# Parking the scores of the last three dense tiles in DRAM, searching them beside the gate matrix, and moving the point that holds the gathers

## The chip, the cores and the metric

The kernel runs on one core of one Trainium2 chip. The metric is the device time of one execution in microseconds; of several runs the median counts. One execution was also profiled, and all rows below come from that one. The engines are called PE (TensorE, with its weight loads as PEld), DVE (VectorE), ACT (ScalarE), POOL (GpSimd) and SP (SyncE, which here only issues transfers); a "q" behind a name is that engine's instruction queue, where waits and issues stand.

## What is computed

One decoder layer on 1024 tokens of width 1024: retention and stick-breaking attention, an output projection, and then a feed-forward layer of 16384 single-neuron experts (PEER). The change lies in that last part:

```python
qry = (ht @ w_query).reshape(T, PEER_HEADS, 2, PEER_HALF)
sub_scores = jnp.einsum('thpc,hpkc->thpk', qry, sub_keys).astype(jnp.float32)
top_s, top_i = lax.top_k(sub_scores, K)                 # 8 heads x 2 halves, 128 keys, 16 kept
cand_s = top_s[:, :, 0, :, None] + top_s[:, :, 1, None, :]
best_s, best_c = lax.top_k(cand_s.reshape(T, PEER_HEADS, K * K), K)
gate = jax.nn.softmax(best_s, axis=-1)
# for each token: 128 experts (8 heads x 16)
a = jnp.einsum('pd,ped->pe', xb, expert_down[ids])
act = jax.nn.gelu(a, approximate=False) * gates
y = jnp.einsum('pe,ped->pd', act, expert_up[ids])
```

So each token has 16 rows of 128 scores, of each of which the 16 largest are wanted, and then a second choice among sums of pairs.

## The kernel before

The 1024 tokens are eight tiles of 128. Tiles 0 to 3 are *gathered*: for each of a token's 128 experts one indirect DMA on POOL fetches 128 rows of `down` (`row("down", j)`, line 778), DVE takes the inner product (line 789); then the same with `up` (line 778 again, and DVE's accumulation at line 799). That is 256 gathers of 512 KB for a tile, 1024 in all, numbered n = 256 t + j (128 more for `up`), through five buffers `g`. Tiles 4 to 7 are *dense*: all experts are computed for 512 tokens with matmuls, and a gate matrix that is zero for experts that were not chosen picks the right ones.

The order in which work is traced: three segments of attention and routing (`seg_gen`, tiles 0, 1 to 3, 4 to 7), then `dense`, then the gathers of all four tiles. A planner that simulates the engines orders the instructions of each engine: what is traced earlier goes first where both could go, so gathers fill gaps. Each engine then runs its list in order.

*Routing in a segment.* For each quarter g of the query weights (`stream(A["wq"], ...)`) PE forms queries and scores; ACT copies the scores of one half-head, for all tiles of the segment, into a tile `sco` of the segment's pool `v` (nine buffers). For a tile that has an entry in `sc_d` the scores go to DRAM with one transfer of 64 KB for each tile and half-head (line 649); before the change that is tile 3 alone. For the other tiles `top16` (lines 672 to 676, five DVE instructions) searches them at once. `topk` (lines 694 to 751) makes the second choice, with small DVE instructions and copies on ACT in between. For tile 4 (t0 == NG) it is called in four pieces of two heads, one behind each quarter; for tiles 5, 6 and 7 it is handed on in the list `late`, for eight heads at a time.

*The dense part.* First six experts' first halves (`stage1_ahead`, lines 836 to 839, their splits at line 824 on POOL), and `to_slots` for tile 4. Then the gate matrix, in 16 pieces c of 32 tokens: for each of eight steps q one DVE comparison (line 876, 128 x 1024), one POOL product (line 877), one ACT copy, PE products (line 883) and ACT copies out, and the piece is written to DRAM (`g_d`). Tile 4 takes pieces 0 to 3, tile 5 pieces 4 to 7, and so on. The pieces also carry 24 further `stage1_ahead` between them, whose splits (line 824) run on DVE. The late `topk` of tiles 5, 6 and 7 are traced before pieces 1, 5 and 9 (`LC`). Then come 32 groups of four blocks of 128 experts each: gate product (line 920), split (line 923), and the second matmuls (lines 946 to 948; 32 of line 946 in each group). Tile 3's parked scores are read back (line 680) and searched two heads at a time before groups 4, 5, 6 and 7 (`todo`, `route_late`).

*The hold.* Gathers with n from 480 to 495 may not be issued on POOL before the last POOL product of gate piece 4 (`HOLD`, `HOLD_C`, `tc.issue_after`); later ones follow them through the five buffers.

Of the kernel before, what the change touches and what calls it, by code (L numbers as in the profile page):

```python
# [23 lines left out]
NT = 8  # L24
SEGS = [(0, 1), (1, 3), (4, 4)]
NG = 4
# [4 lines left out]
LC = 1, 5, 9  # L31

RET = "h0 K h1 t0 Q h2 t1 V h3 t2 | t3"
HOLD, HOLD_C = 480, 4
LT0, LATE = 3, (4,)
# [19 lines left out]
def tile_kernel(ctx, tc, A, out):  # L55
# [10 lines left out]
    sc_d = {t: dram.tile([128, 16, 128], F32, name=f"scd{t}") for t in range(LT0, NG)}  # L66
# [163 lines left out]
    def seg_gen(phase, t0, nt, hooks):  # L230
# [403 lines left out]
        for g in range(4):  # L634
            ky = V((128, 4, 128))
            SP.dma_start(ky, A["keysT"][:, 4 * g:4 * g + 4])

            def ev_q(i, acc):
                q = V()
                copy(q[:, :n], acc[:, :n])  # L640
                tp = pstile("tp", 2)
                for j in range(nt):
                    PE.matmul(tp[:, 128 * j:128 * j + 128], q[:, 128 * j:128 * j + 128], ky[:, i], start=True, stop=True)
                sco = V()
                copy(sco[:, :n], tp[:, :n])
                for j in range(nt):
                    s, h, p = sco[:, 128 * j:128 * j + 128], (4 * g + i) // 2, i % 2
                    if t0 + j in sc_d:
                        SP.dma_start(sc_d[t0 + j][:, 2 * h + p, :], s)
                    else:  # L650
                        top16(kp, tv[j][:, h, p], ix[j][:, h, p], s)

            stream(A["wq"], 512 * g, hT[t0], ev_q, True)
            if t0 in (0, NG):
                topk(kp, tv[0][:, 2 * g:2 * g + 2], ix[0][:, 2 * g:2 * g + 2], t0, 2 * g, 2)
        if t0 == 0:
            return []
        late = []
        for i in own[t0 == NG:]:
            f = lambda i=i: topk(kp, tv[i], ix[i], t0 + i, 0, 8)  # L660
            if t0 < NG:
                f()
            else:
                late.append(f)
        return late
# [143 lines left out]
    def dense(Hhi, Hlo, dp, kpg, late):  # L809
# [50 lines left out]


        iota8 = iota128[:, None, :, :].to_broadcast([128, 2, 128, 4])
        for c in range(TD // CT):
            for k in range(1, 4):
                if c == LC[k - 1]:
                    late[k - 1]()
# [30 lines left out]
        todo = {g: (t, 2 * k) for t, gg in zip(sc_d, LATE) for k, g in enumerate(range(gg, gg + 4))}  # L897
# [84 lines left out]
    with tc.tile_pool(name="tp", bufs=1) as tp_:  # L982
        kpg = tc.tile_pool(name="kp", bufs=1, side="right")
        kp = kpg.__enter__()
        with tc.tile_pool(name="att", bufs=1) as att:
# [4 lines left out]
            with tc.tile_pool(name="wp", bufs=1) as wp, tc.tile_pool(name="up", bufs=13) as up, \  # L990
                    tc.tile_pool(name="vp", bufs=9) as vp:
                late = []
                for s in SEGS:
                    late = seg_gen((wp, tp_, up, vp, kp), *s, late)
        with tc.tile_pool(name="gr", bufs=1) as gr, tc.tile_pool(name="dp", bufs=1, reuse_waits="tile") as dp:
            hold = dense(*hT[NG], dp, kpg, late)
# [61 lines left out]
```

## Time and profile before

| | us |
|---|---|
| median of three runs | 3145.78 |
| the three runs | 3138.63 to 3146.57 |
| the profiled execution | 3142.38 |
| its span | 3140.7 |

Busy shares of the span: PE 86%, DVE 80%, POOL 61%, ACT 41%; mean granted PE clock 0.906. A busy share over the whole span mixes stages; the tables by stretch are what is read below. The stretches, in us from the span's start: 1320 to 1432 the query weights of the third segment, 1432 to 1476 the gap until the gate matrix, 1476 to 1792 the gate matrix, from 1840 the groups.

### The profile page before, as it was taken

To read this page: it belongs to the slowest core of one execution; us is meant where nothing else is said; L and a number is where in the kernel's file an instruction comes from. 1 tells how busy PE (TensorE), PEld (TensorE's weight loads), DVE (VectorE), ACT (ScalarE), POOL (GpSimd) and SP (SyncE) were. 2 spreads that over 40 slices of the span, in tenths; PEclk is the share of its full clock that TensorE was granted. 3 is DMA by queue.
4 is the path that set the end of the run, shared out by engine and by line. 5 is a ranking of instruction groups with operands and counts; after the bars stand their busy time and mean duration, and the time that the engine had idled before them with its cause. 6 is when DMAs were issued, how large, how long until landed. Compare 5 with 4: busy or idle time off the path is not lost.

```text
span 3140.7 us, 38200 instructions
## 1 busy us (share of the span) xinstructions
PE 2691.9 (86%) x12308; PEld 2091.2 (67%) x12308; DVE 2514.9 (80%) x4677; ACT 1287.2 (41%) x2255; POOL 1914.5 (61%) x1590
## 2 busy tenths in 40 slices
PE   6957877787987787794889999789999999999995
PEld 2454654576765345583778887667877788888884
DVE  2269879799988898899989867997666677788778
ACT  1223334244333363432666644444444444444441
POOL 1125775677787567751478757545666666766664
PEclk9978985888998588896999999899999999999998
DMA  8788877998787777960379889778998999998997
GB/s 321 251 302 275 299 236 255 319 358 291 252 289 246 251 237 261 325 228 28 115 286 353 320 303 348 255 256 314 324 333 306 331 341 338 338 338 331 352 338 261
DMA packets 299881, 903.36 MB, mean 288 GB/s; under 512 B 34840, under 2 KB 102424, under 8 KB 279200
## 3 DMA queue, kind: packets, MB, share of 16 engines
q0 software_dynamic: 147456, 536.94, 48.3%
q1 hardware_dynamic: 152224, 363.98, 32.2%
q8 instruction: 97, 1.59, 0.2%
q14 instruction: 104, 0.85, 0.1%
HBM read 848.34 MB, written 52.45 MB: 287 GB/s over the span
## 4 chain that ended last, share of the span: by engine, by line
PE 34%; DVE 27%; DMA 15%; issue 12%; POOL 9%; ACT 3%; SPq 1%; POOLq 0%; DVEq 0%; ACTq 0%
DMA g<-in_up_dram,ids 6%; DVE g L789 6%; POOL g L778 5%; PE tp L837 4%; PE tp L838 4%; PE tp L839 4%; PE acc L948 4%; PE acc L946 3%; PE acc L947 3%; DVE gy L799 3%; DMA g<-in_down_dram,ids 3%; DVE p L876 2%; PE acc L263 2%; POOL wlo L273 2%; DVE oh L736 1%
## 5 line engine op out<-in xcount | busy, mean ns | idle before, releaser
L778 POOL DMA_INDIRECT g<-in_down_dram,ids x512 | 549.7, 1074 | 446.0 <-DVE g L789 229.9
L778 POOL DMA_INDIRECT g<-in_up_dram,ids x512 | 562.2, 1098 | 383.4 <-DVE gy L799 253.7
L799 DVE SCALAR_TENSOR_TENSOR gy<-g,a,gy 128x1024 f32<-128x1024 f32 x508 | 651.3, 1282 | 100.2 <-DMA g<-in_up_dram,ids 94.8
L789 DVE SCALAR_TENSOR_TENSOR g<-g,gy 128x1024 f32<-128x1024 f32 x512 | 614.3, 1213 | 107.6 <-DMA g<-in_down_dram,ids 105.4
L837 PE MATMUL tp<-Thi,dhi 128*128 128x512 f32 x1024 | 407.7, 398 | 37.0 <-ACT dhi L71 30.5
L946 PE MATMUL acc<-u,p 128*128 128x512 f32 x1024 | 399.1, 399 | 27.0 <-ACT p L71 14.1
L948 PE MATMUL acc<-u,p 128*128 128x512 f32 x1024 | 386.5, 396 | 26.0 <-DVE p L923 26.0
L839 PE MATMUL tp<-Thi,dlo 128*128 128x512 f32 x1024 | 403.7, 395 | 3.1 <-DVE dlo L824 2.5
L947 PE MATMUL acc<-u,p 128*128 128x512 f32 x1024 | 405.0, 397 | 0.0
L838 PE MATMUL tp<-Tlo,dhi 128*128 128x512 f32 x1024 | 404.7, 395 | 0.0
L824 POOL TENSOR_TENSOR u<-raw,u 128x1024 fp32r<-128x1024 f32 x128 | 306.7, 2409 | 18.1 <-ACT u L71 16.4
L273 POOL TENSOR_TENSOR wlo<-wraw,whi 128x512 fp32r<-128x512 f32 x182 | 235.8, 1306 | 79.2 <-ACT whi L71 71.2
L824 DVE TENSOR_TENSOR dlo<-raw,dhi 128x1024 fp32r<-128x1024 f32 x122 | 200.2, 1642 | 87.3 <-ACT dhi L71 87.3
L71 ACT ACTIVATE whi<-wraw 128x512 fp32r<-128x512 f32 x208 | 128.3, 629 | 336.6 <-PE acc L283 117.6
L837 PEld LDWEIGHTS tp<-Thi,dhi 128*128 128x128 f32 x1024 | 195.5, 191 | 79.7 <-ACT dhi L71 32.6
L946 PEld LDWEIGHTS acc<-u,p 128*128 128x128 f32 x1024 | 197.1, 192 | 73.7 <-ACT p L71 17.3
L948 PEld LDWEIGHTS acc<-u,p 128*128 128x128 f32 x1024 | 194.8, 191 | 72.4 <-DVE p L923 32.1
L282 PE MATMUL acc<-wlo,Thi 128*128 128x512 f32 x504 | 212.5, 422 | 30.6 <-POOL wlo L273 30.5
L71 ACT ACTIVATE yacc<-acc 128x512 f32<-128x512 f32 x186 | 108.3, 592 | 296.2 <-PE acc L948 295.0
L839 PEld LDWEIGHTS tp<-Thi,dlo 128*128 128x128 f32 x1024 | 195.2, 191 | 44.8 <-DVE dlo L824 3.5
L947 PEld LDWEIGHTS acc<-u,p 128*128 128x128 f32 x1024 | 197.1, 192 | 41.4
L838 PEld LDWEIGHTS tp<-Tlo,dhi 128*128 128x128 f32 x1024 | 195.6, 191 | 39.3
(271 smaller groups left out, 5076.1 us busy)
## 6 DMA issues: line engine op xcount, KB each, us to landing
raw<-in_downT_dram SPq DMA_DIRECT2D x64, 1024.0 KB
raw<-in_up_dram SPq DMA_DIRECT2D x64, 1024.0 KB
gd<-u SPq DMA_DIRECT2D x32, 1024.0 KB
gm<-gd SPq DMA_DIRECT2D x512, 64.0 KB
wraw<-in_w_in_dram SPq DMA_DIRECT2D x56, 512.0 KB
u<-in_ada_w_dram SPq DMA_DIRECT2D x46, 512.0 KB
wraw<-in_wq_dram SPq DMA_DIRECT2D x32, 512.0 KB
u<-in_w_in_dram SPq DMA_DIRECT2D x28, 512.0 KB
```

The source lines that it names most:

```text
L71: ACT.activation(out_, in_, AF.Copy, scale=scale)
L273: (POOL if kt else DVE).tensor_sub(lo, raw, hi.bitcast(F32))
L778: POOL.indirect_dma_start(out=g, out_offset=None, in_=A[src], in_offset=bass.IndirectOffsetOnAxis(ap=groups[j // m][0][:, j % m:j % m + 1] ...
L789: DVE.scalar_tensor_tensor(g, g, 1.0, hp, op0=OP.mult, op1=OP.mult, accum_out=a[:, j:j + 1])
L799: DVE.scalar_tensor_tensor(y, g, a[:, j:j + 1], y, op0=OP.mult, op1=OP.add)
L824: eng.tensor_sub(lo, raw, hi.bitcast(F32))
L837: PE.matmul(a, dhi[:, sl], Hhi[:, kt], start=kt == 0, stop=False)
L838: PE.matmul(a, dhi[:, sl], Hlo[:, kt], start=False, stop=False)
L839: PE.matmul(a, dlo[:, sl], Hhi[:, kt], start=False, stop=kt == KT - 1)
L946: PE.matmul(y, phi[:, sl], uhi[:, ds_], start=st and b == 0, stop=False, skip_group_check=True)
L947: PE.matmul(y, phi[:, sl], ulo[:, ds_], start=False, stop=False, skip_group_check=True)
L948: PE.matmul(y, plo[:, sl], uhi[:, ds_], start=False, stop=sp and b == GB - 1, skip_group_check=True)
```

## The change

The scores of tiles 5, 6 and 7 now go to DRAM as tile 3's do (48 more transfers of 64 KB, in the third segment), and no `top16` runs for them there; tile 4's are searched at once as before, and its `topk` runs in two pieces of four heads. In the gate matrix a step `late_step(t, k)` is traced before pieces 0 to 11: for tile 5 in pieces 0 to 3, tile 6 in 4 to 7, tile 7 in 8 to 11. Steps k = 0 to 3 each read four half-heads' scores (256 KB) back into a buffer `p2` and search them; step 4 is the `topk` of eight heads. By `LC` piece 0 of four has step 0, piece 1 steps 1 and 2, piece 2 step 3, piece 3 step 4. The hold now stands before gathers 512 to 527 (the first of tile 2) and waits for the last POOL product of piece 10. Tile 3's late routing comes before groups 4, 7, 10 and 13 (`LS` = 3).

```diff
--- before.py
+++ after.py
@@ -28,11 +28,11 @@
 GB = 4
 CT = 32
 NB = 128
-LC = 1, 5, 9
+LC = 0, 1, 1, 2, 3
 
 RET = "h0 K h1 t0 Q h2 t1 V h3 t2 | t3"
-HOLD, HOLD_C = 480, 4
-LT0, LATE = 3, (4,)
+HOLD, HOLD_C = 512, 10
+LT0, LATE, LS = 3, (4,), 3
 
 PM, NS, NSE, NSL = 2, 8, 6, 6
 NP = 36
@@ -63,7 +63,8 @@
 
     x1_d = [dram.tile([128, D], F32, name=f"x1d{i}") for i in range(NT)]
     h2_d = [dram.tile([128, D], F32, name=f"h2d{i}") for i in range(NG)]
-    sc_d = {t: dram.tile([128, 16, 128], F32, name=f"scd{t}") for t in range(LT0, NG)}
+
+    sc_d = {t: dram.tile([128, 16, 128], F32, name=f"scd{t}") for t in (*range(LT0, NG), *range(NG + 1, NT))}
     a_d = [dram.tile([128, TD], F32, name=f"ad{i}") for i in range(NP - NS)]
     g_d = [dram.tile([128, NB, CT], F32, name=f"gd{i}") for i in range(TD // CT)]
 
@@ -651,18 +652,15 @@
                         top16(kp, tv[j][:, h, p], ix[j][:, h, p], s)
 
             stream(A["wq"], 512 * g, hT[t0], ev_q, True)
-            if t0 in (0, NG):
-                topk(kp, tv[0][:, 2 * g:2 * g + 2], ix[0][:, 2 * g:2 * g + 2], t0, 2 * g, 2)
+            nh = {0: 2, NG: 4}.get(t0)
+            if nh and (2 * g + 2) % nh == 0:
+                hs = slice(2 * g + 2 - nh, 2 * g + 2)
+                topk(kp, tv[0][:, hs], ix[0][:, hs], t0, hs.start, nh)
         if t0 == 0:
             return []
-        late = []
         for i in own[t0 == NG:]:
-            f = lambda i=i: topk(kp, tv[i], ix[i], t0 + i, 0, 8)
-            if t0 < NG:
-                f()
-            else:
-                late.append(f)
-        return late
+            topk(kp, tv[i], ix[i], t0 + i, 0, 8)
+        return []
 
     def flat(x):
         return x.rearrange("p a b -> p (a b)")
@@ -806,7 +804,7 @@
         DVE.tensor_add(x1, x1, g2)
         SP.dma_start(out[t * 128:(t + 1) * 128], x1)
 
-    def dense(Hhi, Hlo, dp, kpg, late):
+    def dense(Hhi, Hlo, dp, kpg, kp):
 
         def U8(shape, dt):
             return dp.tile(shape, dt, name="u8", tag="u8", bufs=6)
@@ -858,12 +856,27 @@
             stage1_ahead(n)
         to_slots(NG, *route[NG])
 
+        lt = {}
+
+        def late_step(t, k):
+
+            if k == 0:
+                lt[t] = (kp.tile([128, 8, 2, 16], F32, name="tvl", bufs=1), kp.tile([128, 8, 2, 16], U32, name="ixl", bufs=1))
+            v, ix = lt[t]
+            if k == 4:
+                return topk(kp, v, ix, t, 0, 8)
+            sc = P2([128, 4, 128], F32)
+            SP.dma_start(sc, sc_d[t][:, 4 * k:4 * k + 4, :])
+            for j in range(4):
+                h = 2 * k + j // 2
+                top16(kp, v[:, h, j % 2], ix[:, h, j % 2], sc[:, j])
+
 
         iota8 = iota128[:, None, :, :].to_broadcast([128, 2, 128, 4])
         for c in range(TD // CT):
-            for k in range(1, 4):
-                if c == LC[k - 1]:
-                    late[k - 1]()
+            for k in range(len(LC)):
+                if c % 4 == LC[k] and c < TD // CT - 4:
+                    late_step(NG + 1 + c // 4, k)
             rb, rg = route[NG + c * CT // 128]
             st = [U8([128, NB // 2, CT], F32) for _ in range(2)]
             for q in range(CT // 4):
@@ -894,7 +907,7 @@
         kpg.__exit__(None, None, None)
         dp2g = tc.tile_pool(name="dp2", bufs=1, side="right")
         dp2 = dp2g.__enter__()
-        todo = {g: (t, 2 * k) for t, gg in zip(sc_d, LATE) for k, g in enumerate(range(gg, gg + 4))}
+        todo = {g: (t, 2 * k) for t, gg in zip(range(LT0, NG), LATE) for k, g in enumerate(range(gg, gg + 4 * LS, LS))}
         held = [pstile("acc", 4) for _ in range(2)]
         hh = len(held) // 2
         yacc = dp2.tile([128, TD // 128 - hh, D], F32, name="yacc")
@@ -989,11 +1002,10 @@
             POOL.memset(state, 0.0)
             with tc.tile_pool(name="wp", bufs=1) as wp, tc.tile_pool(name="up", bufs=13) as up, \
                     tc.tile_pool(name="vp", bufs=9) as vp:
-                late = []
                 for s in SEGS:
-                    late = seg_gen((wp, tp_, up, vp, kp), *s, late)
+                    seg_gen((wp, tp_, up, vp, kp), *s, [])
         with tc.tile_pool(name="gr", bufs=1) as gr, tc.tile_pool(name="dp", bufs=1, reuse_waits="tile") as dp:
-            hold = dense(*hT[NG], dp, kpg, late)
+            hold = dense(*hT[NG], dp, kpg, kp)
 
     for t in range(NG):
```

## Rows read from the trace of the kernel before

**Rows 1.** The page, part 1: busy time, share, instructions

```profile
PE 2691.9 (86%) x12308; PEld 2091.2 (67%) x12308; DVE 2514.9 (80%) x4677; ACT 1287.2 (41%) x2255; POOL 1914.5 (61%) x1590
```

**Rows 2.** Windows; columns: PE, PEld, DVE, ACT, POOL busy, clock, DMA share, GB/s

```profile
1366.00:1432.00 66.00, 57.42 (x273) 47.51 (x271) 66.00 (x405) 22.73 (x41) 17.63 (x14) 0.91 0.33 120
1432.00:1476.00 44.00, 12.51 (x40) 9.28 (x41) 41.88 (x266) 7.98 (x12) 6.19 (x3) 0.56 0.07 25
1476.00:1564.00 88.00, 78.83 (x411) 65.88 (x410) 79.78 (x229) 53.10 (x94) 39.28 (x28) 0.94 0.30 111
1564.00:1727.00 163.00, 146.62 (x888) 128.10 (x887) 144.15 (x147) 112.89 (x256) 129.35 (x108) 0.96 0.82 309
1727.00:1792.00 65.00, 63.13 (x409) 56.27 (x407) 58.03 (x63) 47.17 (x109) 51.45 (x45) 1.00 0.88 318
...
2515.00:3032.00 517.00, 516.88 (x2280) 427.66 (x2279) 406.12 (x492) 223.27 (x334) 345.14 (x264) 1.00 0.92 340
```

**Rows 3.** Waits from 1335 to 1500: total, times, longest

```profile
PE tp L837 <- ACT dhi L71: 28.7, 1, 28.7
```

**Rows 4.** Timeline of ACT from 1431: start, us, what, idle before

```profile
1431.91 0.60 ACT L71 ACTIVATE v<-tp 128x512 f32<-128x512 f32 x1 [2.23 <-PE tp L643]
...
1459.42 1.99 ACT L71 ACTIVATE dhi<-raw 128x1024 fp32r<-128x1024 f32 x2
...
1476.23 0.38 ACT L71 ACTIVATE rb<-acc 128x256 bf16<-128x256 f32 x1
```

**Rows 5.** Windows of line 778, the gathers' issues: POOL busy (count), clock, DMA

```profile
1366.00:1595.00 229.00, 0.41 (x1) 0.87 0.29 108
1595.00:1727.00 132.00, 41.47 (x35) 0.95 0.89 336
1727.00:1792.00 65.00, 16.77 (x14) 1.00 0.88 318
```

**Rows 6.** Timeline of DVE, the last accumulation of a gather

```profile
3132.50 1.29 DVE L799 SCALAR_TENSOR_TENSOR gy<-g,a,gy 128x1024 f32<-128x1024 f32 x1 [2.22 <-DMA g<-in_up_dram,ids]
```

**Rows 7.** Line 948: duration ns min/median/max, first and last start

```profile
L948 PE MATMUL acc<-u,p x1024: 387/389/797, 1840.8 to 3111.5; 128*128 128x512 f32 x171
```

**Rows 8.** Timeline of DVE, instructions of the search start to start

```profile
1380.92 0.07 DVE L674 MATCH_VALUE_LOAD s<-tv,v 128x8 f32 x1
...
1381.17 0.08 DVE L674 MATCH_VALUE_LOAD s<-tv,v 128x8 f32 x1
...
1381.43 0.47 DVE L675 MAX8 tv<-s 128x8 f32<-128x128 f32 x2
```

**Rows 9.** DVE groups by line, 1476 to 1792: count, busy, mean ns

```profile
L876 DVE TENSOR_TENSOR p<-iota,rb 128x1024 bf16<-128x1024 bf16 x128 | 134.1, 1072 | 16.4 <-POOL p L877 11.2 <-PE acc L883 2.3 <-ACT rb L71 1.4
...
L824 DVE TENSOR_TENSOR dlo<-raw,dhi 128x1024 fp32r<-128x1024 f32 x25 | 38.5, 1539 | 7.4 <-ACT dhi L71 7.4
```

**Rows 10.** Same view: first and last group of topk's 29

```profile
L736 DVE TENSOR_TENSOR oh<-oh 128x1024 bf16<-128x1024 bf16 (+2 forms) x18 | 12.4, 691 | 0.3
...
L698 DVE TENSOR_TENSOR cs<-tv 128x64 f32<-128x64 f32 x2 | 0.4, 219 | 0.0
```

**Rows 11.** Timeline of DVE, topk of tile 4's last piece

```profile
1460.46 4.89 DVE L736 TENSOR_TENSOR oh<-oh 128x256 bf16<-128x256 bf16 x3
```

**Rows 12.** Timeline of POOL, the same stretch

```profile
1460.59 4.69 POOL L824 TENSOR_TENSOR dlo<-raw,dhi 128x1024 fp32r<-128x1024 f32 x2 [50.68 <-ACT dhi L71]
```

**Rows 13.** SP's own waits, 640 to 800, second segment's score transfers

```profile
SPq L649 <- ACT v L71: 23.0, 16, 1.9
```

**Rows 14.** Windows of line 946 (32 make a group): PE, PEld, clock, DMA

```profile
1935.00:2111.00 176.00, 55.00 (x129) 26.86 (x129) 0.89 0.77 267
...
2191.00:2465.00 274.00, 95.94 (x256) 48.73 (x256) 0.99 0.89 319
```

**Rows 15.** Windows of line 876, pieces 5 and 6 (eight steps each)

```profile
1594.40:1621.40 27.00, 10.10 (x8) 0.87 0.88 331
1621.40:1643.20 21.80, 6.30 (x8) 0.93 0.81 302
```

## Prediction, made before the change was run

> **What bounds the kernel now.** I read the page's busy times first: PE 86% and DVE 80% of 3140.7 us [rows 1]. Neither is full, so the question is which one is full where, and the table by stretch answers it. From 2515 to 3032 PE is busy 516.9 of 517 us: the groups run at PE's pace [rows 2]. From 1366 to 1432 DVE is busy 66.0 of 66, and from 1432 to 1476 it is busy 41.9 of 44 while PE has 12.5 of 44 at a granted clock of 0.56, which is a mixture of the two levels 1.2 and 2.4 GHz, and memory moves 25 GB/s [rows 2]. That gap is DVE's: the searches of four tiles and the second choices of tile 4 stand there. The waits name it from PE's side: once, 28.7 us for ACT's first split of an expert block [rows 3]; and ACT's list shows that it came to that split only at 1459.4, behind copies that wait for DVE's `topk`, though the last scores had been copied out at 1431.9 [rows 4]. The gate matrix from 1476 to 1792 is mixed: at first DVE has 79.8 of 88 (the late `topk` of three tiles), then PE 146.6 of 163 and DVE 144.2 of 163, and in the last four pieces PE 63.1 of 65 [rows 2].
>
> The end is shared. PE's last matmul starts at 3111.5 [rows 7], the last gather is added at 3132.5 [rows 6]; so the gathers are some 20 us the later, and a gain on PE counts only if the gathers keep up.
>
> **The change part by part, (a): the start of the gate matrix.** The searches of 48 of 64 tile-half-heads leave the segment. A search is three instructions of the kind load and find (or replace), 0.25 us start to start, and two MAX8 at 0.235, together 1.22 us [rows 8]; 48 make 58.6 us of DVE. The segment's stream then ends with PE's own work: PE lost some 7 us of its 1366 to 1432 to such waits (57.4 busy of 66 [rows 2], part of which is other idling), so the last scores are out at about 1425 in place of 1432. Behind that come one search (1.2), the first part of a `topk` of four heads (about 12, an estimate: a little over half of the 20 us that I take below for eight heads), and what stood from the halving steps to ACT's `rb`: 1476.2 - 1460.5 = 15.7 [rows 4, 11], of which 4 were a block that I come to, with 2 more for twice as many heads, so 14. That gives 1425 + 1 + 12 + 14, about 1452, for `rb`, and 1453 for the first comparison, in place of 1476.6: 24 us earlier. PE meanwhile does the first six expert blocks, of which only two had been done before.
>
> Bounds of (a): 15 and 28 us earlier. The better one is a chain that is 4 us shorter, by the overlap of its search with the stream. The worse one has a row: three halving steps of a `topk` took 4.89 us on DVE from 1460.5 [rows 11], although steps of up to four times their width take 0.69 in the mean [rows 10]; exactly beside them POOL made two expert splits, 4.69 us [rows 12]. After the change four more such splits, 2.35 us each, can fall beside the last `topk`: 9 us, which takes the gain of (a) from 24 to 15. [...]
>
> The 48 score transfers go through SP's list, past the loads of query weights. The second segment has 16 such, waiting 23.0 us in all for ACT, at most 1.9 each [rows 13]. The loads of weights behind them have two buffers, and and a wait of 1.9 us is short beside a quarter of the stream; I cost this at nothing, and without that cover at up to 2 us for each quarter, 8 us.
>
> **(b): pieces 0 to 11 with the searches in them.** What is late next is DVE. Its work for these twelve pieces, without a gather: 96 comparisons at 1.05 us (134.1 us by 128) 100.6; 18 splits at 1.54, 27.7 [rows 9]; 48 searches 58.6 [rows 8]; three `topk` of eight heads, 29 groups that add up to 71.6 us busy of which neighbours overlap [rows 10], so 60, between 50 and 72. Together 247, between 237 and 259. DVE was busy 100%, 95% and 91% in its three fullest stretches [rows 2]; I take 95%, which gives about 258 us (260 by that share), that is 21.5 for a piece. PE needs less there: its 88% in 1564 to 1727 included 13 pieces less three. So piece 12 begins at 1453 + 258 = 1711, where it began at 1727: **16 us earlier**. With 237 and no idle time it would be 41 earlier; with 259 at the 88% of 1564 to 1727, and (a) at its worse bound, 29 later (1462 + 294 = 1756).
>
> **(c): the hold.** Before, gathers stopped with the 480th, one was issued from 1366 to 1595, then 35 to 1727 and 14 to 1792 [rows 5]: 530 by the end of the gate matrix. After, 32 more may go before the hold. They fit where the searches were: 32 accumulations at 1.28 are 41 us of DVE out of the 58.6 freed, and memory was at 120 and 25 GB/s there [rows 2]. Then nothing until piece 10 ends, at about 1453 + 258 x 11/12 = 1690. From there to the end at 1711 + 65 = 1776 the old pace of 14 in 65 us gives 18, less some three while tile 7's `topk` holds DVE: 527. Queued behind the held gather on POOL are only products and later gathers; the planner puts products ahead. Three gathers fewer than before cost at the end of the kernel about 1.5 us each: **5 us later**. Bounds: 0, and 27 if none of the 18 goes (18 at 1.5).
>
> **(d): tile 3's routing, every third group.** From 1935 to 2111, 129 matmuls of line 946 stand for four groups, 43.7 us each; from 2191 to 2465, 256 for eight, 34.3 each [rows 14]: 9.4 us for each late routing, 38 for four. Set apart, each has quiet groups behind it in which DVE can catch up, which would leave perhaps 3 us each: 26 to 37 gained. Against that, the first of the four stood behind quiet groups and was no cheaper, since its instructions go ahead of that group's gate products; then nothing is gained. I stand nearer to the second: **8 us earlier**, between 0 and 37.
>
> **Sum.** From piece 12 on nothing else changes. Minus 16, minus 8, plus 5: 19 us, 3142.4 to about 3123 against the profiled execution; against the median of 3145.8, which lies 3.4 us above it, **3127 us**.
>
> **The rivals.** *Slower: the searches overload the gate matrix.* They are traced ahead of the piece that they stand before, so that piece's comparisons wait, then POOL's products, then PE, whose granted clock falls after idle time (0.87 in piece 5 [rows 15]). The point that decides is a piece of 22.8 us: (1727.1 - 1453) by 12. Pieces 5 and 6, where other DVE work stood between, took 27.0 and 21.8 [rows 15], 24.4 in the mean; twelve such are 293, piece 12 begins at 1746, 19 later, and with (c), and (d) at nothing, 3145.8 + 19 + 5 is 3170; with (d) 3162. For it: PE's long waits in that stretch. Against: in those two pieces 16 gathers took DVE, which the new hold keeps out.
>
> *No change: the gathers bind.* The 32 early gathers don't find DVE free, or the 18 don't go before 1776; 18 missing at 1.5 us are 27 us, which eat the 24 of (a, b, d): about 3148, and between 3137 and 3154. That is also the case that the change doesn't do what it says, as the hold would be a later stop and no earlier start. For it: the gathers already end last [rows 6].
>
> *Much faster.* DVE keeps busy without a gap and the late routing apart costs 3 us each: 41 and 26 or more against 5 to 10, about 3085 to 3100.
>
> **How the numbers follow.** The forecast, 3110 to 3140: 0.45. Slower, 3155 to 3175: 0.20. Gathers bind: 0.17. Much faster, below 3110: 0.18. A measurement of this kernel tells 0.3% (9.4 us) from no change. Faster by more than that is the much faster case and all but 0.05 of the forecast, 0.58; within it the gathers' case and that 0.05, 0.22; slower 0.20. The range leaves out a tenth at each end: 3090 to 3162.
>
> **What would show it.** The first comparison at about 1453 (a); PE's wait of 28.7 us gone; piece 12 at about 1711, pieces 0 to 11 at 21.5 us each with DVE at 95% (b); 32 gathers before the first comparison, some 15 between piece 10 and the end of the gate matrix (c); groups 4, 7, 10 and 13 at 40 to 44 us and the others at 34 (d); the last gather still some 20 us behind the last matmul. The prediction is wrong if pieces take over 22.8 us, or if the last gather falls much further behind PE.

## The result, and the profile after

| | before | after |
|---|---|---|
| median of six runs, us | 3139.2 | 3161.3 |
| the runs | 3132.5 to 3146.6 | 3147.9 to 3172.1 |
| span of the profiled execution | 3140.7 | 3162.5 |

The changed kernel is slower: the medians are 22 us apart, and the recorded ratio is 1.0084, with a 95% interval of 1.0058 to 1.0109. I had forecast 19 us faster.

Where the time went is read from the same views as before. Line numbers have moved by some lines; L889 is the comparison of the gate matrix (was L876), L776 the gather (L778), L761 the transposes of a tile's routing to slots, L735 the sum that ends each of the two halves of a second choice, L961 the last matmul of a group (L948).

First the stretches of the kernel after; columns: stretch, length, busy PE, PEld, DVE, ACT and POOL (counts), granted clock, DMA share, GB/s. They answer to [rows 2].

```profile
1366.00:1432.00 66.00, 48.88 (x223) 38.28 (x221) 61.19 (x160) 18.86 (x32) 40.56 (x38) 0.91 0.89 294
1432.00:1463.00 31.00, 15.59 (x54) 11.51 (x55) 29.27 (x98) 9.61 (x12) 9.41 (x4) 0.72 0.64 231
1463.00:1572.00 109.00, 91.45 (x504) 79.52 (x504) 80.12 (x247) 61.28 (x123) 42.13 (x34) 0.90 0.35 130
1572.00:1660.00 88.00, 66.00 (x399) 57.22 (x398) 78.26 (x258) 53.98 (x114) 37.63 (x32) 0.90 0.43 161
1660.00:1712.00 52.00, 48.06 (x300) 41.68 (x299) 47.83 (x143) 33.43 (x77) 28.44 (x24) 1.00 0.51 194
1712.00:1785.00 73.00, 30.51 (x154) 25.77 (x152) 65.92 (x168) 24.75 (x46) 48.12 (x45) 0.72 0.89 317
1785.00:1848.00 63.00, 52.89 (x335) 47.18 (x336) 60.14 (x69) 40.30 (x95) 51.98 (x47) 0.95 0.93 329
2569.00:3086.00 517.00, 516.58 (x2279) 427.19 (x2278) 406.78 (x462) 222.37 (x332) 350.09 (x266) 1.00 0.92 343
```

Three things stand there. The segment's end does what the change wanted: from 1366 to 1432 memory moves 294 GB/s in place of 120, and the gate matrix begins at 1463 in place of 1476. The groups are unchanged (516.6 of 517 for PE). But from 1712 to 1785 PE is busy 30.5 of 73 us, and it is not full from 1572 to 1660 either. In those stretches DVE is not full all the time (80 of 109, 78 of 88, 66 of 73): it is not simply overloaded.

The waits of the kernel after from 1463 to 1800 say who waits for whom: total, times, longest.

```profile
POOL p L890 <- DVE p L889: 94.1, 64, 6.4
...
PE acc L761 <- DVE ii L735: 68.7, 5, 34.6
POOL p L890 <- PE acc L896: 40.5, 4, 16.6
```

And PE's timeline names the three long ones, each in front of the first of the three transposes for the next tile (start, length, idle time before and what ended it):

```profile
1558.29 0.45 PE L761 MATMUL acc<-ident,ii 128*128 128x128 f32 x1 [15.81 <-DVE ii L735]
...
1647.63 0.45 PE L761 MATMUL acc<-ident,ii 128*128 128x128 f32 x1 [17.18 <-DVE ii L735]
...
1754.29 0.45 PE L761 MATMUL acc<-ident,ii 128*128 128x128 f32 x1 [34.56 <-DVE ii L735]
```

So PE stood 68.7 us for the sums of second choices, in pieces 3, 7 and 11. Those pieces took 39.6, 38.0 and 72.8 us, the other nine of the first twelve 12 to 28 (first comparison to first comparison).

The gathers of the kernel after (windows of L776, POOL busy and count; they answer to [rows 5]):

```profile
1366.00:1463.00 97.00, 25.52 (x26) 0.85 0.81 274
1463.00:1712.00 249.00, 0.00 (x0) 0.92 0.41 154
1712.00:1785.00 73.00, 39.71 (x36) 0.72 0.89 317
1785.00:1848.00 63.00, 18.61 (x16) 0.95 0.93 329
```

The early ones are there, none is issued while the hold stands, and then 36 fall into piece 11. By the end of the gate matrix 563 are issued, where it was 529. The end itself, line 961's summary and two rows of DVE's timeline, against [rows 6, 7]:

```profile
L961 PE MATMUL acc<-u,p x1024: 387/389/796, 1898.7 to 3157.5; 128*128 128x512 f32 x171
```

```profile
3112.20 1.28 DVE L797 SCALAR_TENSOR_TENSOR gy<-g,a,gy 128x1024 f32<-128x1024 f32 x1
...
3158.69 0.69 DVE L969 TENSOR_TENSOR x1f<-x1f,yacc 128x512 f32<-128x512 f32 x1
```

The last gather is added at 3113.5 (20 us earlier than before), PE's last matmul ends at 3157.9 (46 us later). The order of the two has turned round. PE's 46 us are: gate matrix begun 13 earlier, pieces 0 to 11 72 us longer (322 in place of 250), pieces 12 to 15 2 shorter, and 11 us less from there to the last matmul. Of these 46, the first 22 only closed the gap to the gathers; the rest, and what follows the last matmul, is the 22 us of the result.

### The profile page after: what moved, and what is told of

Its sections match the earlier page's. It is cut to its first block, busy times and chain, and to the rows that moved or that the text cites. A ratio compares the mean times of both kernels' runs of the same rounds, so it can differ in the third digit from the quotient of the medians.

```text
span 3162.5 us, 38251 instructions
## 1 busy us (share of the span) xinstructions
PE 2679.8 (85%) x12308; PEld 2083.4 (66%) x12308; DVE 2519.9 (80%) x4619; ACT 1289.4 (41%) x2249; POOL 1910.3 (60%) x1590
## 4 chain that ended last, share of the span: by engine, by line
PE 39%; DVE 26%; DMA 14%; issue 10%; POOL 6%; ACT 3%; SPq 1%; POOLq 0%; DVEq 0%; ACTq 0%
PE tp L835 5%; DVE g L787 5%; PE tp L836 5%; PE tp L837 5%; PE acc L961 5%; PE acc L959 5%; PE acc L960 5%; POOL g L776 4%; DMA g<-in_down_dram,ids 3%; DVE gy L797 3%; DMA g<-in_up_dram,ids 2%; DVE p L889 2%; DMA raw<-in_downT_dram 2%; PE acc L264 2%; POOL wlo L274 1%
## 5 line engine op out<-in xcount | busy, mean ns | idle before, releaser
L776 POOL DMA_INDIRECT g<-in_up_dram,ids x512 | 559.3, 1092 | 412.1 <-DVE gy L797 204.6
L776 POOL DMA_INDIRECT g<-in_down_dram,ids x512 | 556.8, 1088 | 390.1 <-DVE g L787 235.8
L961 PE MATMUL acc<-u,p 128*128 128x512 f32 x1024 | 383.2, 394 | 18.5 <-DVE p L936 18.5
L822 POOL TENSOR_TENSOR u<-raw,u 128x1024 fp32r<-128x1024 f32 x128 | 308.7, 2425 | 48.1 <-ACT u L72 43.2
L890 POOL TENSOR_TENSOR p<-p,rg 128x512 f32<-128x512 bf16 x128 | 146.3, 1151 | 147.5 <-DVE p L889 98.7
L961 PEld LDWEIGHTS acc<-u,p 128*128 128x128 f32 x1024 | 194.2, 190 | 62.6 <-DVE p L936 22.2
```

Source lines behind the costliest of these rows:

```text
L776: POOL.indirect_dma_start(out=g, out_offset=None, in_=A[src], in_offset=bass.IndirectOffsetOnAxis(ap=groups[j // m][0][:, j % m:j % m + 1] ...
L822: eng.tensor_sub(lo, raw, hi.bitcast(F32))
L961: PE.matmul(y, plo[:, sl], uhi[:, ds_], start=False, stop=sp and b == GB - 1, skip_group_check=True)
```

## The experiments

All times of this table are of the profiled execution, us from the span's start; "starts" is the first comparison of the gate matrix, "piece 12" its comparison number 97, "gate end" the start of the last one, "issued" the gathers issued by then. The last column is the recorded ratio to the kernel before on the same chip, with its 95% interval; it is not the plain quotient of the two medians and lies up to 0.002 from it.

| kernel | starts | piece 12 | gate end | issued | PE's last ends | last gather added | ratio |
|---|---|---|---|---|---|---|---|
| before | 1477 | 1727 | 1791 | 529 | 3112 | 3134 | 1 |
| after | 1463 | 1785 | 1847 | 563 | 3158 | 3114 | 1.0084 (1.0058 to 1.0109) |
| e1_hold12 | 1461 | 1745 | 1814 | 531 | 3134 | 3151 | 1.0077 (1.0058 to 1.0097) |
| e2_lead | 1463 | 1732 | 1802 | 539 | 3126 | 3126 | 1.0020 (0.9995 to 1.0044) |
| e3_nochain | 1457 | 1714 | 1799 | 544 | 3141 | 3135 | 1.0064 (1.0036 to 1.0092) |
| e4_ls1 | 1464 | 1785 | 1848 | 563 | 3169 | 3125 | 1.0155 (1.0125 to 1.0185) |
| e5_searchback | 1507 | 1748 | 1816 | 542 | 3147 | 3148 | 1.0058 (1.0033 to 1.0084) |
| e6_spread | 1471 | 1723 | 1786 | 529 | 3117 | 3133 | 1.0023 (0.9997 to 1.0049) |
| e7_defer | 1468 | 1745 | 1814 | 548 | 3139 | 3123 | 1.0035 (1.0004 to 1.0067) |
| e8_hold | 1501 | 1747 | 1816 | 542 | 3144 | 3145 | 1.0067 (1.0039 to 1.0096) |
| e9_oldhold | 1446 | 1838 | 1902 | 604 | 3201 | 3071 | 1.0246 (1.0201 to 1.0291) |
| e10_lead_oldhold | 1457 | 1838 | 1904 | 611 | 3215 | 3052 | 1.0262 (1.0221 to 1.0302) |
| e11_before_480_10 | 1460 | 1703 | 1773 | 509 | 3087 | 3145 | 1.0059 (1.0037 to 1.0082) |
| e12_before_512_4 | 1509 | 1765 | 1829 | 564 | 3160 | 3117 | 1.0107 (1.0071 to 1.0142) |
| e13_actq | 1471 | 1792 | 1854 | 563 | 3157 | 3113 | 1.0132 (1.0092 to 1.0171) |
| e14_actq_lead | 1462 | 1732 | 1804 | 539 | 3125 | 3126 | 1.0016 (0.9987 to 1.0045) |
| e15_actq_lead_480 | 1464 | 1734 | 1802 | 507 | 3132 | 3197 | 1.0196 (1.0158 to 1.0234) |

Theory C: the second choice of a tile is a chain that now stands right in front of the tile's first piece, and PE waits for it. Theory L: DVE is simply full. Theory H: the gathers released by the new hold take DVE away.

### The changed kernel with one thing altered

**e1_hold12.**

```diff
-HOLD, HOLD_C = 512, 10
+HOLD, HOLD_C = 512, 12
```

> The changed kernel with the hold moved from piece 10 to piece 12, so that gathers from 512 on are released behind the second choice of tile 7 and not in front of it. In the changed kernel pieces 3, 7 and 11, the last before a new tile, take 39.6, 38.0 and 72.8 us, and the others 12 to 28. Theory H (the released gathers take DVE from tile 7's second choice): piece 11 falls from 72.8 to about 38, like 3 and 7, the gate matrix ends some 33 us earlier (1847 to about 1814), and the median falls from 3161 to 3130 or, if the gathers that start later become the last to end, to 3145. Theory C (what costs is only the chain of the second choice in front of each new tile): piece 11 stays above 60 and the median within 8 us of 3161.

Windows of L889 for piece 11 in the kernel after and in e1 (length, DVE busy, clock, DMA):

```profile
1712.50:1785.30 72.80, 7.08 (x8) 0.72 0.89 319
```

```profile
1708.60:1745.20 36.60, 7.73 (x8) 0.77 0.28 108
```

Piece 11 falls from 72.8 to 36.6 us, like pieces 3 and 7, and the gate matrix ends 33 us earlier: theory H holds for half of piece 11. PE's last matmul comes 24 us earlier. But the last gather is now added at 3151, 18 us behind PE, and the median stays at 3158, beyond the 3145 that I had allowed for that case: what PE gained the gathers lost.

**e2_lead.**

```diff
-LC = 0, 1, 1, 2, 3
+LC = 0, 0, 1, 1, 2
```

> The changed kernel with the search steps one piece earlier (0, 0, 1, 1, 2): the second choice of a tile is traced two pieces ahead of its first use and not one. Theory C (the chain of the second choice is exposed because it starts too late): pieces 3 and 7 fall from 39.6 and 38.0 to 20 to 25, the pieces before them grow by less than that, piece 8 starts 15 to 30 us earlier than 1660, and the median falls to 3130 to 3150. Theory L (DVE is simply full): the same time is only moved from pieces 3 and 7 into pieces 0 to 2 and 4 to 6, piece 8 starts within 8 us of 1660 and the median is within 8 us of 3161.

The waits from 1455 to 1790:

```profile
PE acc L761 <- DVE ii L735: 29.9, 2, 15.0
```

Median 3142 in place of 3161. The wait for the second choices falls from 68.7 to 29.9 us and the gate matrix ends at 1802 in place of 1847. Piece 8 begins 20 us earlier, and up to there no gather is issued in either kernel: this is theory C, not L (up to 5 us of it are searches of tile 5 that now lie ahead of the first comparison). The other 25 us are not theory C's alone. Tile 7's second choice now ends at 1714, just when the hold lets go, so that 9 gathers fall into pieces 10 and 11 in place of 36, and piece 11 takes 18.5 us in place of 72.8 (piece 10 takes 36.9 in place of 17.4). By the end of the gate matrix 24 gathers fewer are issued, which at some 1.2 us each is 29 us of DVE that this kernel does later. The two waits that are left stand in pieces 6 and 10, two pieces ahead of the first use.

**e3_nochain.**

```diff
-        elif not piece:
-            to_slots(t, ii, gt)
...
-            rb, rg = route[NG + c * CT // 128]
+            rb, rg = route[NG]
```

> The changed kernel with all DVE work of the second choices kept, but their result unused: pieces 4 to 15 use the routing of tile 4, and the transposes of tiles 5, 6 and 7 are left out, so the output is not the reference's. This takes away PE's wait for the second choice, not DVE's load. Theory C: pieces 3 and 7 fall to 16 to 24 us, piece 11 below 50, the gate matrix ends 50 us or more earlier than 1847, and the median falls below 3135. Theory L: pieces 3 and 7 stay above 30, or the others grow by as much, and the gate matrix ends after 1830.

Windows of e3, pieces 0 to 11 and 12 to 15 (columns as above):

```profile
1456.00:1713.70 257.70, 225.22 (x1283) 194.05 (x1283) 229.04 (x715) 159.02 (x336) 126.31 (x108) 0.95 0.48 178
1713.70:1799.00 85.30, 71.07 (x399) 61.81 (x397) 82.91 (x124) 53.07 (x113) 62.32 (x54) 0.87 0.79 289
```

With nobody waiting for the second choices, pieces 0 to 11 take 257 us in place of 322, and piece 12 begins at 1714. Pieces 3 and 7 took 24.5 and 24.1 us, at the edge of what theory C gave, and the gate matrix ends 48 us earlier. But the 65 us of pieces 0 to 11 are not all waiting. Since nothing needs it, the end of tile 7's second choice has slipped behind piece 12 (its last sum on DVE's timeline):

```profile
1781.45 0.38 DVE L735 TENSOR_TENSOR ii<-oh 128x128 f32<-128x128 bf16 x1
```

Pieces 12 to 15 take 85 us here in place of 62, and piece 11 has 10 gathers in place of 36. The whole gate matrix takes 342 us in place of 384: 42 us less, with 19 gathers fewer issued by its end. The median fell by only 10 us, to 3151, not below 3135, and the intervals of the two ratios overlap: from the gate matrix's end to PE's last matmul this kernel took 1341 us, the kernel after 1311. Why its groups were slower no run tells.

**e4_ls1.**

```diff
-LT0, LATE, LS = 3, (4,), 3
+LT0, LATE, LS = 3, (4,), 1
```

> The changed kernel with tile 3's late routing back before groups 4, 5, 6 and 7. If spreading it over groups 4, 7, 10 and 13 gains what I forecast (8 us, up to 37), the median rises from 3161 to 3169 or more. If each late routing costs the same wherever it stands (from group 3 to group 17 the two kernels took 530 and 529 us), it stays within 8 us of 3161.

3178 against 3161: in the changed kernel, where PE ends last, the spread is worth 17 us by the medians, and 11 us of PE's end in the profiled executions.

**e7_defer** (with the edit of e2).

```diff
-            to_slots(t, ii, gt)
+            route[t] = ii, gt
...
+            if c and c % 4 == 0:
+                to_slots(NG + c // 4, *route[NG + c // 4])
             rb, rg = route[NG + c * CT // 128]
```

> The changed kernel with the search steps one piece earlier and the three transposes of a tile's routing traced in front of that tile's first piece, not behind its second choice. With the steps one piece earlier alone, PE still waited 14.9 and 15.0 us for the sums of the second choice in pieces 6 and 10, which nothing needed before pieces 8 and 12. If PE's place in its own list is what costs, those waits go, pieces 6 and 10 fall from 32.7 and 36.9 to 18 to 22, the gate matrix ends 20 to 30 us earlier than 1802, and the median falls from 3142 to 3110 to 3125, below the kernel before. If DVE's load sets the pace, the gate matrix ends within 10 us of 1802.

```profile
PE acc L761 <- DVE ii L735: 8.0, 3, 4.0
```

The wait is all but gone (8.0 us from 1460 to 1810), and yet the gate matrix ends at 1814, not earlier than 1802, and the median is 3144. Pieces 6 and 10 do fall to 16 and 17 us, but 7 and 11 grow to 39 and 47. Where the planner put the second choices instead is a new order of DVE's list; the time has moved, and the forecast for this run failed. So it is not shown that PE's place in its list is what costs: e2's two remaining waits cost nothing that e7 could get back.

### The parts alone, in the kernel before

**e8_hold.**

```diff
-HOLD, HOLD_C = 480, 4
+HOLD, HOLD_C = 512, 10
```

> The kernel before with one edit, the hold of the gathers (before 512, on piece 10, in place of 480 on piece 4). If the 32 gathers let go earlier only take DVE from the searches in the segment, the gate matrix starts later than 1476 by up to 40 us and the median rises by 10 to 30 us. If they find idle time, as the sum for the change took it, the median is within 8 us of the kernel before.

Waits of e8 from 1380 to 1510, and its windows:

```profile
PE tp L837 <- ACT dhi L71: 42.7, 1, 42.7
```

```profile
1366.00:1440.00 74.00, 39.68 (x189) 32.56 (x188) 74.00 (x273) 16.83 (x29) 36.94 (x37) 0.77 0.77 250
1440.00:1500.00 60.00, 13.78 (x47) 10.49 (x48) 58.61 (x365) 10.80 (x16) 5.86 (x3) 0.54 0.22 82
```

Here the 32 early gathers meet the searches: DVE is busy 74.0 of 74 and 58.6 of 60, PE's wait for the first expert block grows from 28.7 [rows 3] to 42.7, and the gate matrix begins at 1501. 21 us slower. The loads of that block are late as well (SP issues them at 1447.4 in place of 1403.6), but they are not what PE waits for: ACT comes to the first split without idle time, right behind a copy of the second choice.

```profile
1483.69 0.63 ACT L71 ACTIVATE oh<-ab 128x512 bf16<-128x512 f32 x1 [0.72 <-DVE ab L717]
1484.22 1.99 ACT L71 ACTIVATE dhi<-raw 128x1024 fp32r<-128x1024 f32 x2
```

**e12_before_512_4** and **e11_before_480_10** take the two numbers of the hold apart.

```diff
-HOLD, HOLD_C = 480, 4
+HOLD, HOLD_C = 512, 4
```

> The kernel before, with the hold in front of gather 512 in place of 480, still released by piece 4 (the early start alone). If the early gathers are what costs in the segment, the gate matrix begins near 1501 in place of 1476 and ends 20 us or more later than 1790, but with some 32 gathers more done; the median is then within 10 us of the kernel before if the gathers set its end, and 15 us or more above it if PE does.

```diff
-HOLD, HOLD_C = 480, 4
+HOLD, HOLD_C = 480, 10
```

> The kernel before, with gathers from 480 on held until piece 10 in place of piece 4 (the later stop alone, without 32 early gathers). The gate matrix should begin at about 1476 as before, run without gathers up to piece 10 and end 20 to 40 us earlier than 1790, with some 30 gathers fewer; PE's last matmul should come earlier than 3112 and the last gather later than 3134, so that the median rises by 10 to 40 us if the gathers set the end.

The early start alone: gate matrix from 1509 to 1829 with 564 gathers, PE's end 48 us later, the gathers' 17 earlier, and PE sets the end. The later stop alone: PE's last matmul 25 us earlier, but the last gather at 3144.5, and the gathers set the end:

```profile
3143.24 1.29 DVE L799 SCALAR_TENSOR_TENSOR gy<-g,a,gy 128x1024 f32<-128x1024 f32 x1 [2.28 <-DMA g<-in_up_dram,ids]
```

Between these two the kernel before stands where both ends are near each other. The gate matrix of e11 began at 1460, 16 us earlier than I had expected, and its end moved by only 18 us.

**e6_spread.**

```diff
-... for k, g in enumerate(range(gg, gg + 4))}
+... for k, g in enumerate(range(gg, gg + 12, 3))}
```

> The kernel before with one edit, tile 3's late routing before groups 4, 7, 10 and 13. In the changed kernel the opposite edit cost 17 us (3178 against 3161). If spreading is worth that by itself, this is 10 to 20 us below the kernel before. If its end is set by the gathers (last added at 3133.8, PE's last matmul over at 3111.9), a gain on PE is worth less, and it is within 8 us of the kernel before.

Same as before (0.9997 to 1.0049): the gathers set the end there, and PE's last matmul came 5 us later, not earlier. What e4 showed for the changed kernel does not hold here.

**e5_searchback** is the kernel before with e8's and e6's edits and tile 4's second choice in two pieces, that is the change without the parking.

```diff
-HOLD, HOLD_C = 480, 4
+HOLD, HOLD_C = 512, 10
...
-            if t0 in (0, NG):
-                topk(kp, tv[0][:, 2 * g:2 * g + 2], ...)
+            nh = {0: 2, NG: 4}.get(t0)
+            if nh and (2 * g + 2) % nh == 0:
+                ...
```

> The changed kernel with its first part undone: the scores of tiles 5, 6 and 7 are searched in the segment and their second choices traced before pieces 1, 5 and 9, as before; two pieces of four heads for tile 4, the new hold and the spread late routing stay. If the parking is what makes the change slow, this is some 20 us or more below the changed kernel's 3161, at 3120 to 3140. If the hold or the spread do it, it stays above 3150.

3152, above the 3150 that was to speak for the hold, though by less than its runs scatter (3143 to 3164), and with the hold's late start (1507). Without the parking the change is slow for another reason than with it.

### Does the hold cost the same where the searches have left?

**e9_oldhold**, and **e10_lead_oldhold** with e2's edit as well.

```diff
-HOLD, HOLD_C = 512, 10
+HOLD, HOLD_C = 480, 4
```

> The changed kernel with the hold as it was before (480, released by piece 4). The hold alone, put into the kernel before, cost 20 us (3156 against 3135), because its 32 early gathers took DVE from the searches in the segment and the gate matrix began at 1501 in place of 1476. In the changed kernel those searches are gone. If the early gathers still cost DVE there, the gate matrix begins 10 to 30 us before 1463. The gathers of pieces 4 to 11 then meet the searches and second choices in the gate matrix: theory C (chains in front of a new tile, stretched by gathers) has piece 7 go from 38.0 to 50 or more and the median at 3150 to 3165; theory H (the hold is the whole loss) has the median at 3130 to 3142.

> The same with the search steps one piece earlier. One piece of lead took 19 us off the changed kernel (3142 against 3161). If the lead and the old hold add up, the median falls to 3115 to 3130, below the kernel before. If DVE's total from 1320 to the end of the gate matrix sets the pace, whatever the order, it stays at 3133 to 3150.

Waits of e9 from 1440 to 1850, and its gathers in pieces 4 to 11 (1550.8 to 1837.9):

```profile
PE acc L761 <- DVE ii L735: 93.3, 4, 42.0
```

```profile
1550.80:1837.90 287.10, 123.93 (x109) 0.76 0.86 306
```

Much slower, 3212 and 3220, and further than either theory went. The gate matrix begins 17 us earlier, but 109 gathers then fall into pieces 4 to 11, beside searches and second choices; pieces 7 and 11 take 69 and 78 us and PE waits 93.3 us. A lead of one piece doesn't help there. So the later stop is needed once the searches are in the gate matrix.

**e13_actq, e14_actq_lead, e15_actq_lead_480.** The start of the gate matrix came 10 us later than forecast. In the kernel after ACT waits for the first expert block, whose loads SP issues at 1431.7 (in the kernel before at 1403.6); rows of ACT and of SP:

```profile
1440.63 2.00 ACT L72 ACTIVATE dhi<-raw 128x1024 fp32r<-128x1024 f32 x2 [14.25 <-DMA raw<-in_downT_dram]
```

```profile
1419.40 8.31 SPq L650 DMA_DIRECT2D scd<-v  x12
...
1431.74 1.54 SPq L817 DMA_DIRECT2D raw<-in_downT_dram  x3
```

```diff
-                        SP.dma_start(sc_d[t0 + j][:, 2 * h + p, :], s)
+                        (ACT if t0 == NG else SP).dma_start(sc_d[t0 + j][:, 2 * h + p, :], s)
```

(e14 with e2's edit as well, e15 with `HOLD = 480` as well.)

> The changed kernel with the 48 score transfers of the third segment issued from ACT's list in place of SP's. In the changed kernel the loads of the first expert blocks stood behind the last twelve score transfers in SP's list, were issued at 1431.7 in place of 1403.6, and PE waited 16.0 us for the split that needs them. If SP's list is the cause of that wait, the loads are issued before 1415, the wait falls to 5 us or less, the gate matrix begins 5 to 12 us before 1463, and with the three waits for the second choices unchanged the median falls from 3161 to 3148 to 3158. If the loads wait for room in memory and not for their turn, nothing moves.

> The same with the search steps one piece earlier. If the two causes add up, the median is 5 to 12 us below the 3142 of the lead alone, at 3130 to 3137, level with the kernel before. If DVE's total sets the end, it stays at 3138 to 3146.

> The same with the hold in front of gather 480 in place of 512, still released by piece 10: without the 32 early gathers the segment's DVE is free and the gate matrix begins 10 to 25 us earlier, at 1430 to 1450, PE's last matmul comes 15 to 30 us earlier than with the early gathers, and the last gather 20 to 50 us later than PE's. If the early gathers found idle time, PE's end does not move and the median is 15 us or more worse; if DVE is what is conserved, PE's end moves as far forward as the gathers' end moves back.

SP's list in e13:

```profile
1437.74 0.33 SPq L801 DMA_DIRECT2D g<-x1d  x1
1439.95 0.33 SPq L229 DMA_DIRECT2D g<-row_gate  x1
1440.33 1.41 SPq L817 DMA_DIRECT2D raw<-in_downT_dram  x3
```

The score transfers' place in SP's list is not the only cause: with them on ACT's list the loads are issued later still, at 1440.3, and the kernel isn't faster. In e13 the loads stand right behind those for the end of tile 1, whose last gathers are the early ones (480 to 511). In e15 neither the early gathers nor the score transfers stand in front of them in SP's list. SP's own waits name what holds SP in e13 and then in e15 (total, times, longest):

```profile
SPq L801 <- DMA g<-in_up_dram,ids: 23.9, 1, 23.9
```

```profile
SPq L817 <- DMA scd<-v: 26.6, 2, 18.9
```

In e13 it is the last gathers of tile 1; in e15 it is the landing of the score transfers. e9 has the score transfers in SP's list, but not the early gathers. There the loads follow the last score transfer at once:

```profile
1414.11 9.19 SPq L650 DMA_DIRECT2D scd<-v  x12
1423.34 1.38 SPq L817 DMA_DIRECT2D raw<-in_downT_dram  x3
```

So three things stand before these loads, and where one is taken away another binds: the turn behind the score transfers, the end of tile 1, and the landing of the scores. No run takes away all three.

e14 is level with the kernel before (3136 against 3133), as e2 was; I don't take the 6 us between them as shown. e15 also bears on the hold: without the early gathers the gate matrix begins at 1463.6, no earlier than with them (1462.3), PE's end is no earlier (3132), and the last gather is added at 3197. By this pair the early gathers find idle time in the changed kernel. By two others they cost something: without them e9's gate matrix begins 17 us before that of the kernel after, and e10's 6 us before that of e2. What they cost there stays open; in the kernel before they do cost (e8, e12).

## Why the prediction was wrong, step by step

**The step that failed is (b): its 95%**, the share of the time that DVE was to be busy, and with it that nothing would have to wait for the second choices. Its sum of loads was not too low. In e1, where no gather is issued before piece 12, DVE is busy 236.1 us in pieces 0 to 11, and I had written 247 (4 of the 48 searches lie ahead of piece 0, some 5 us); yet these pieces take 284.8 us, a share of 83%. In the kernel after it is 272.1 of 322, 85%. Windows of pieces 0 to 11 of e1 and of the kernel after (columns as above):

```profile
1460.50:1745.30 284.80, 224.59 (x1304) 195.42 (x1304) 236.07 (x747) 169.97 (x352) 118.77 (x98) 0.90 0.39 148
```

```profile
1463.00:1785.00 322.00, 236.03 (x1351) 204.19 (x1350) 272.12 (x811) 173.45 (x357) 156.32 (x134) 0.88 0.52 191
```

So 258 became 285 with the waits in it, and the gathers released into piece 11 make it 322. The 95% had come from the gap before the gate matrix; the gate matrix itself showed 91, 88 and 89% [rows 2]. That e3 took 257 us, next to my 258, is luck: DVE was busy 229.0 of them, 89%, and part of tile 7's second choice came later.

What (b) left out is an order. I put the three second choices into the sum as 60 us of DVE work that could lie anywhere. Before the change it could: the scores had long been searched, and all three stood in the first pieces, well ahead of tiles 5, 6 and 7. After it, a tile's second choice can begin only when the tile's last search is done, and that is in the piece just before the one that needs it. It is a chain through DVE and ACT; in piece 3, rows of DVE's timeline (the last find of tile 5's search, and the sums of the two halves of its second choice):

```profile
1535.02 0.28 DVE L674 FIND_INDEX8 ixl<-tvl,s 128x8 uint32<-128x128 f32 x1
...
1557.75 0.39 DVE L735 TENSOR_TENSOR ii<-oh 128x128 f32<-128x128 bf16 x1
...
1567.50 0.39 DVE L735 TENSOR_TENSOR ii<-oh 128x128 f32<-128x128 bf16 x1
```

That is 23 us to the first sum and 33 to the second, more than the 18 or so that one of pieces 3 to 11 took before. PE's first transpose for tile 5 waits for the first sum, and POOL and ACT then wait for PE. PE's 68.7 us of waits are the trace of it; e2, which starts the chain a piece earlier, more than halves them and takes 19 us off the median. (b) also read PE's share from 1564 to 1727 as 88%; it is 146.62 of 163, 90%, for nine pieces [rows 2]. Nothing in the sum rests on that.

**(c) was wrong about the release.** Whether the early gathers cost nothing, as I had written, is not settled (e15 against e9). But the hold lets go just when tile 7's second choice begins. I had taken three gathers off for that; instead 36 gathers went into piece 11 and doubled it (72.8 against 36.6 in e1). The sum counted what the second choice does to the gathers and not what the gathers do to the second choice. No row shows its 1.5 us for a gather fewer either: e15 against e14, whose gate matrices end alike, has 32 gathers fewer and its last gather 71 us later, 2.2 us each.

**(a)** gave 24 us, bounds 15 to 28, and it was 13: the searches are gone from the segment, and PE's wait of 28.7 us became one of 16.0, for a load. I had costed the score transfers at nothing against the loads of weights, and had not looked at the loads of expert blocks that follow, nor at the end of tile 1 that the early gathers bring in front of them (e13, e9, e15).

Some of tile 4's last second choice did stand beside POOL's splits, as my worse bound had it (up to 9 us), and took some 6 us more for it, about 2 each for L732, L707 and a halving step. Rows of DVE (L732 away from a split, then beside one; L707 beside one) and of POOL:

```profile
1449.55 0.69 DVE L732 TENSOR_TENSOR oh<-oh,ixf 128x1024 bf16<-128x1024 bf16 x1
...
1454.91 2.74 DVE L732 TENSOR_TENSOR oh<-oh,ixf 128x1024 bf16<-128x1024 bf16 x1
```

```profile
1444.19 2.37 DVE L707 TENSOR_SCALAR pq<-px 128x64 uint32<-128x64 uint32 x1
```

```profile
1441.82 4.69 POOL L822 TENSOR_TENSOR dlo<-raw,dhi 128x1024 fp32r<-128x1024 f32 x2 [13.64 <-ACT dhi L72]
...
1454.73 2.38 POOL L822 TENSOR_TENSOR dlo<-raw,dhi 128x1024 fp32r<-128x1024 f32 x1 [8.22 <-ACT dhi L72]
```

One input alone does not keep an instruction clear of POOL: L707 has one, and it took 0.21 us in piece 3 at twice the width. The searches were not slowed by POOL's products: a find took 284 ns in the mean in pieces 0 to 10, and 285 in the segment of the kernel before. Of L671 in pieces 0 to 10, and of the same find in the kernel before from 1320 to 1476, count, busy and mean ns:

```profile
L671 DVE FIND_INDEX8 ixl<-tvl,p 128x8 uint32<-128x128 f32 x44 | 12.2, 284 | 0.0
```

```profile
L673 DVE FIND_INDEX8 ix<-tv,v 128x8 uint32<-128x128 f32 x64 | 17.4, 285 | 0.0
```

The Trainium skill (SBUF — State Buffer, section "Who interferes with whom") has it that a DVE instruction with at most one SBUF input does not contend with GpSimd, except in the 2-port modes, which take the ports that the two share and which it says `tensor_scalar` can enter. The finds agree with that, and L707 with the exception.

**(d)** was right in sign for the changed kernel and too small, 17 us in place of 8 (e4), and worth nothing in the kernel before (e6). In total from group 3 to group 17 the kernels before and after took 530 and 529 us; the gain is one that stands only in comparison with the changed kernel unspread.

**The sum.** Minus 16 became plus 58 at piece 12 (1785 against 1727). The sum also took the gathers' end as the end throughout; the 46 us by which PE ends later count from 22 us on, since the gathers had been that far behind.

**The rivals.** The slower one had the right sign and size (3162 to 3170 against 3161), and its point of 22.8 us for a piece was passed: 322 by 12 is 26.8. Its mechanism was not the one: pieces with searches took 12 to 28 us, pieces with second choices 38 and more. The gathers' rival did not happen; they ended 44 us before PE. My chances gave 0.20 to slower. That 3161.3 lies inside my range of 3090 to 3162 is luck: its upper end came from this rival and not from the forecast's mechanism.

**What is settled and what is not.** Shown: the gathers released in front of tile 7's second choice double piece 11 (e1); a second choice begun a piece earlier brings piece 8 forward by 20 us and keeps most of those gathers out of its way (e2); and the change is then level with the kernel before (e2, e14), not better. Not shown: why no order gets below it. In the table a later gate end mostly goes with more gathers issued by then (e11, before, e8, e12), as if DVE's work between 1320 and 1800 were what is conserved; that is argued from four points, not tested. Why e3's groups were slower is open, and so is what the early gathers cost in the changed kernel.

## What to carry to other kernels

Work that is moved beside other work is costed by its load only if nothing waits for its result there; ask first for the last instruction of the chain, what it holds up in an in-order list, and by how much its start now precedes its use. Where two chains of work end near each other (here PE's matmuls and the gathers), a change that favours one is worth at most the gap between them, and a cost on the other begins to count at once or after the gap. A hold that is released at the start of a latency-bound step gives its engine away at the worst moment.

## What the runs showed of the hardware

While PE stood and then worked in piece 11 its granted clock was 0.72 in the mean (the row of 1712 to 1785 above), a mixture of 1.2 and 2.4 GHz, against 1.00 in the stretch from 1660 to 1712, in which it was busy 48.1 of 52 us. How much of the 72.8 us is due to that, no run tells apart.
